# Log-softmax backward on one core: pairs of row groups, half of the sums on ScalarE, and a last store cut in three

## The chip, the core and the metric

The kernel runs on one core of a Trainium2 chip. The core has a vector engine (VectorE, DVE in the profile), a scalar engine (ScalarE, ACT), a general engine (GpSimd, POOL) and a sequencer that only issues transfers and waits (SyncE, SP). Sixteen DMA engines move data between the chip's large memory (HBM) and the core's working memory (SBUF), which has 128 partitions. The metric is device time in microseconds, the median of several executions. Before the change it is 1867.85 us over 9 executions (1866.99 to 1868.25).

## The reference

Inputs are `y` (the output of a log-softmax) and `dy`, each 8 x 1024 x 8192 float32. For each of the 8192 rows:

```
softmax_x = np.exp(y)
sum_dy = np.sum(dy, axis=-1, keepdims=True)
return (dy - softmax_x * sum_dy).astype(np.float32)
```

The two inputs and the output are 268.4 MB each, so 805 MB cross the DMA engines.

## The kernel before

The 8192 rows are cut into G = 32 groups of 256 rows. A group lies on the 128 partitions with R = 2 neighbouring rows per partition, so a partition's share of a group is 2 x 8192 elements, 64 KiB in one run of memory. The program is written out by one Python loop over the groups (L82); a framework inserts the semaphore waits, and each engine carries out its own instructions in the order of the program.

For one group:

- `load_dy` (L43) issues one 8 MiB load of dy into one of two buffers `dy_t` (L45). A `tensor_reduce` on VectorE (L47) sums both rows of every partition in one instruction and negates the sums into `s_t`.
- `load_y` (L56) issues two 4 MiB loads, one for each row of the pair, into two buffers `y_t` (L60). Each partition's piece is 32 KiB.
- `compute` (L64) goes over the two rows in halves of 4096 columns: ScalarE takes Exp in place in `y_t` (L69), then VectorE computes `e * (-sum) + dy` in one `scalar_tensor_tensor` into `dy_t` (L70).
- `store` (L74) writes the `dy_t` buffer back to `out` (L77), 8 MiB in one transfer.

All transfers are issued by SP, in this order once the loop runs: y of this group (two loads), dy of the next group, store of this group, y of the next group, and so on. SP is in order: it stands still at a transfer whose buffer isn't free or whose data isn't computed, and everything behind it in SP's program waits. The dy load of group g+1 takes the buffer of group g-1 and waits until that store has landed. The y loads wait until the computing of the group before has released the buffer.

At the end (L88 to L96) the store of the last but one group is held back and issued after the last y loads, and the last group is stored in two parts, one row of the pair each. The two dy buffers and two y buffers take 192 KiB of each partition.

Of the kernel before, what the change touches and what calls it, by code (L numbers as in the profile page):

```python
# [1 line left out]

# [5 lines left out]


EXP = mybir.ActivationFunctionType.Exp  # L10
ALU = mybir.AluOpType


@with_exitstack
def kernel(
    ctx: ExitStack,
    tc: tile.TileContext,
    y: bass.AP,
    dy: bass.AP,
    out: bass.AP,  # L20
):

    nc = tc.nc
    P = nc.NUM_PARTITIONS
    fp32 = mybir.dt.float32

    N, D = y.flatten_outer_dims().shape
    R = 2  # L30
    G = N // (P * R)
    assert N == G * P * R
    CD = D // 2

    y_v = y.flatten_outer_dims().rearrange("(g p r) d -> g p (r d)", p=P, r=R)
    dy_v = dy.flatten_outer_dims().rearrange("(g p r) d -> g p (r d)", p=P, r=R)
    out_v = out.flatten_outer_dims().rearrange("(g p r) d -> g p (r d)", p=P, r=R)

    dyp = ctx.enter_context(tc.tile_pool(name="dyp", bufs=2))
    yp = ctx.enter_context(tc.tile_pool(name="yp", bufs=R))  # L40
    stats = ctx.enter_context(tc.tile_pool(name="stats", bufs=2))

    def load_dy(g):  # L43
        dy_t = dyp.tile([P, R * D], fp32, name="dy_t")
        nc.sync.dma_start(out=dy_t[:], in_=dy_v[g])  # L45
        s_t = stats.tile([P, R], fp32, name="s_t")
        nc.vector.tensor_reduce(  # L47
            out=s_t[:],
            in_=dy_t[:].rearrange("p (r d) -> p r d", r=R),
            axis=mybir.AxisListType.X,  # L50
            op=ALU.add,
            negate=True,
        )
        return dy_t, s_t

    def load_y(g):  # L56
        y_ts = []
        for r in range(R):
            y_t = yp.tile([P, D], fp32, name="y_t")
            nc.sync.dma_start(out=y_t[:], in_=y_v[g][:, r * D : (r + 1) * D])  # L60
            y_ts.append(y_t)
        return y_ts

    def compute(dy_t, s_t, y_ts):  # L64
        for r in range(R):
            for c in range(0, D, CD):
                e = y_ts[r][:, c : c + CD]
                d = dy_t[:, r * D + c : r * D + c + CD]
                nc.scalar.activation(e, e, EXP)  # L69
                nc.vector.scalar_tensor_tensor(  # L70
                    out=d, in0=e, scalar=s_t[:, r : r + 1], in1=d, op0=ALU.mult, op1=ALU.add
                )

    def store(g, dy_t, parts=1):  # L74
        w = R * D // parts
        for k in range(parts):
            nc.sync.dma_start(  # L77
                out=out_v[g][:, k * w : (k + 1) * w], in_=dy_t[:, k * w : (k + 1) * w]
            )

    cur = load_dy(0)
    for g in range(G):  # L82
        if g < G - 1:
            y_ts = load_y(g)
            compute(*cur, y_ts)
            nxt = load_dy(g + 1)
            if g < G - 2:
                store(g, cur[0])  # L88
                cur = nxt
            else:  # L90
                held, cur = cur, nxt
        else:
            y_ts = load_y(g)
            compute(*cur, y_ts)
            store(g - 1, held[0])
            store(g, cur[0], parts=R)  # L96


# [1 line left out]
_INS = ['y', 'dy']  # L100
_OUTS = [((8, 1024, 8192), 'float32')]


# [23 lines left out]
```

## Time and profile before

| what | value |
|---|---|
| median of 9 executions | 1867.85 us |
| the profiled execution's own time | 1867.34 us |
| its span on the core | 1865.6 us |
| VectorE busy | 1119.2 us (60%) |
| ScalarE busy | 457.1 us (25%) |
| DMA engines' packet time | 100.0% of the span |
| mean rate | 432 GB/s |
| `tensor_reduce`, 128 x 16384 | 32 times, 17220 ns each |
| `scalar_tensor_tensor`, 128 x 4096 | 128 times, 4481 ns each |
| Exp, 128 x 4096 | 128 times, 3608 ns each |

The profile is taken by the hardware on one execution. "Busy" is time in which an engine carries out an instruction. A wait is put down to the work that ended it. The slices cut the span in 40 equal parts; a 9 stands for 90% busy or more. A transfer shows in two places: where SP issues it, and as packets on the 16 DMA engines[...]. The times of single packets are in the trace's packet records.

### The profile page before, as it was taken

What the parts mean: (1) busy time and instruction counts of PE and PEld (TensorE: products, weight loads), DVE (VectorE), ACT (ScalarE), POOL (GpSimd) and SP (SyncE); (2) the same over time, 40 slices, a digit from 0 to 9 for tenths busy, and PEclk for the clock granted to TensorE, in tenths of its full rate; (3) what the DMA queues carried; (4) which work ended last, traced back from release to release, by engine and by line L of the source; (5) the groups of instructions that cost most, each with busy time, mean ns of one, the idle gap of its engine ahead of it and who ended that gap; (6) DMA issues with size and microseconds to landing.
All of it is one profiled execution on the core that took longest, in us unless ns stands there. A gap on an engine that the chain in (4) does not pass through costs nothing.

```text
span 1865.6 us, 712 instructions
## 1 busy us (share of the span) xinstructions
DVE 1119.2 (60%) x160; ACT 457.1 (25%) x129; POOL 0.2 (0%) x4
## 2 busy tenths in 40 slices
DVE  5675555755557555575555755657656576565664
ACT  2023321233212332123321233212332113331132
POOL 0000000000000000000000000000000000000000
DMA  9999999999999999999999999999999999999999
GB/s 427 416 432 434 438 429 429 432 441 433 430 430 432 441 429 436 426 435 438 434 434 427 432 442 433 429 431 435 437 433 436 426 434 439 436 430 431 430 434 399
DMA packets 18582, 805.36 MB, mean 432 GB/s; under 512 B 2064, under 2 KB 2064, under 8 KB 2064
## 3 DMA queue, kind: packets, MB, share of 16 engines
q1 hardware_dynamic: 18576, 805.31, 100.0%
q14 instruction: 6, 0.05, 0.0%
HBM read 536.87 MB, written 268.44 MB: 432 GB/s over the span
## 4 chain that ended last, share of the span: by engine, by line
DMA 74%; DVE 17%; ACT 6%; SPq 1%; issue 1%; DVEq 0%; ACTq 0%
DMA y_t<-in_y_dram 69%; DVE dy_t L70 15%; ACT y_t L69 6%; DMA dy_t<-in_dy_dram 3%; DVE s_t L47 2%; DMA out_dram<-dy_t 1%; SPq L60 1%; SPq L77 1%; DVEq L122 0%; ACTq L69 0%; DVEq L70 0%
## 5 line engine op out<-in xcount | busy, mean ns | idle before, releaser
L70 DVE SCALAR_TENSOR_TENSOR dy_t<-y_t,s_t,dy_t 128x4096 f32<-128x4096 f32 x128 | 568.2, 4481 | 490.2 <-ACT y_t L69 490.0
L69 ACT ACTIVATE y_t<-y_t 128x4096 f32<-128x4096 f32 x128 | 455.9, 3608 | 1375.7 <-DMA y_t<-in_y_dram 1375.7
L47 DVE TENSOR_REDUCE s_t<-dy_t 128x2 f32<-128x16384 f32 x32 | 551.0, 17220 | 232.3 <-DMA dy_t<-in_dy_dram 232.3
L69 ACT ACT_TABLE_LOAD x1 | 1.3, 1283 | 0.7 <-PEq L111 0.7
L111 POOL MEMSET const-bfloat16-1.0<- 128x1 bf16 x1 | 0.1, 102 | 0.0
L111 POOL MEMSET const-uint8-127<- 128x1 uint8 x1 | 0.1, 102 | 0.0
L111 POOL MEMSET const-float32-0.0<- 128x1 f32 x1 | 0.1, 99 | 0.2 <-issue 0.2
L111 POOL MEMSET const-float32-1.0<- 128x1 f32 x1 | 0.1, 99 | 0.0
## 6 DMA issues: line engine op xcount, KB each, us to landing
y_t<-in_y_dram SPq DMA_DIRECT2D x64, 4096.0 KB, 35.9
out_dram<-dy_t SPq DMA_DIRECT2D x2, 4096.0 KB, 22.6
dy_t<-in_dy_dram SPq DMA_DIRECT2D x32, 38.7
out_dram<-dy_t SPq DMA_DIRECT2D x31, 26.1
```

Of the source, the lines that this page charges most:

```text
L47: nc.vector.tensor_reduce(out=s_t[:], in_=dy_t[:].rearrange("p (r d) -> p r d", r=R), axis=mybir.AxisListType.X, op=ALU.add, negate=True,)
L60: nc.sync.dma_start(out=y_t[:], in_=y_v[g][:, r * D : (r + 1) * D])
L69: nc.scalar.activation(e, e, EXP)
L70: nc.vector.scalar_tensor_tensor(out=d, in0=e, scalar=s_t[:, r : r + 1], in1=d, op0=ALU.mult, op1=ALU.add)
L77: nc.sync.dma_start(out=out_v[g][:, k * w : (k + 1) * w], in_=dy_t[:, k * w : (k + 1) * w])
L111: nc = _bacc.Bacc("TRN2", target_bir_lowering=False, num_devices=1)
```

## The change

The groups are taken in pairs. SP's order becomes: dy of the first group, y of the first group, dy of the second, y of the second, store of the first, store of the second. Details:

- There are two dy buffers, `x_ts[0]` for the first group of each pair and `x_ts[1]` for the second, and one y buffer of 2 x 8192 columns for both. Together they again take 192 KiB of each partition.
- y of the first group is one 8 MiB load, 64 KiB per partition. y of the second group is two 4 MiB loads, one for each row; each waits until that row of the first group has been computed, since it overwrites the same half of the y buffer.
- `sums`: VectorE sums the first row of each partition. ScalarE sums the second row, with two Copy instructions of 4096 columns that write into PSUM (their copy isn't used) and accumulate into `half_t`; a small VectorE instruction adds and negates the two halves.
- `compute` cuts a row into pieces of 2048, 3072 and 3072 columns in place of two of 4096.
- The very last store is issued as three transfers: partitions 0 to 14, partitions 15 to 126, and partition 127, whose 64 KiB are cut into 16 runs of 4 KiB.

The instructions on the engines: ScalarE carries out 64 Copies and 192 Exps (128 Exps before), VectorE 32 reduces of 8192 columns, 32 small adds and 192 `scalar_tensor_tensor` (32 reduces of 16384 and 128 before). SP issues 114 transfers (129 before).

```diff
+    PIECES = [(0, 2048), (2048, 5120), (5120, D)]
...
-    dyp = ctx.enter_context(tc.tile_pool(name="dyp", bufs=2))
-    yp = ctx.enter_context(tc.tile_pool(name="yp", bufs=R))
+    x_ts = [pool.tile([P, W], fp32, name=f"x{j}") for j in range(2)]
+    y_t = pool.tile([P, W], fp32, name="y_t")
+    copied = psum.tile([P, H], fp32, name="copied")
...
+    def sums(x):
+        s_t = stats.tile([P, R], fp32, name="s_t")
+        half_t = stats.tile([P, 2], fp32, name="half_t")
         nc.vector.tensor_reduce(
-            out=s_t[:],
-            in_=dy_t[:].rearrange("p (r d) -> p r d", r=R),
-            axis=mybir.AxisListType.X,
-            op=ALU.add,
-            negate=True,
+            out=s_t[:, 0:1], in_=x[:, :D], axis=mybir.AxisListType.X, op=ALU.add, negate=True
         )
+        for h in range(2):
+            nc.scalar.activation(
+                copied[:], x[:, D + h * H : D + (h + 1) * H], COPY, accum_out=half_t[:, h : h + 1]
+            )
+        nc.vector.tensor_scalar(
+            out=s_t[:, 1:2],
+            in0=half_t[:, 0:1],
+            scalar1=half_t[:, 1:2],
+            scalar2=-1.0,
+            op0=ALU.add,
+            op1=ALU.mult,
+        )
+        return s_t
...
+    def load_y(g, lo, hi):
+        nc.sync.dma_start(out=y_t[:, lo:hi], in_=y_v[g][:, lo:hi])
...
+    def compute(x, s_t, r):
+        for b, e in PIECES:
+            cs = slice(r * D + b, r * D + e)
+            nc.scalar.activation(y_t[:, cs], y_t[:, cs], EXP)
+            nc.vector.scalar_tensor_tensor(
+                out=x[:, cs],
+                in0=y_t[:, cs],
+                scalar=s_t[:, r : r + 1],
+                in1=x[:, cs],
+                op0=ALU.mult,
+                op1=ALU.add,
             )
...
+    for g in range(0, G, 2):
+        load_dy(g, x_ts[0])
+        load_y(g, 0, W)
+        s_t = sums(x_ts[0])
+        for r in range(R):
+            compute(x_ts[0], s_t, r)
+        load_dy(g + 1, x_ts[1])
+        s_t = sums(x_ts[1])
+        for r in range(R):
+            load_y(g + 1, r * D, (r + 1) * D)
+            compute(x_ts[1], s_t, r)
+        nc.sync.dma_start(out=out_v[g], in_=x_ts[0][:])
+        if g + 2 < G:
+            nc.sync.dma_start(out=out_v[g + 1], in_=x_ts[1][:])
         else:
+            nc.sync.dma_start(out=out_v[g + 1][0:15], in_=x_ts[1][0:15, :])
+            nc.sync.dma_start(out=out_v[g + 1][15 : P - 1], in_=x_ts[1][15 : P - 1, :])
+            nc.sync.dma_start(
+                out=out_v[g + 1][P - 1 : P].rearrange("p (e w) -> p e w", e=16),
+                in_=x_ts[1][P - 1 : P, :].rearrange("p (e w) -> p e w", e=16),
+            )
```

More of the change, by code (lines that the diff above doesn't have):

```diff
@@ L10 @@
 EXP = mybir.ActivationFunctionType.Exp
+COPY = mybir.ActivationFunctionType.Copy
 ALU = mybir.AluOpType
@@ L30 @@
     R = 2
+    W = R * D
     G = N // (P * R)
-    assert N == G * P * R
-    CD = D // 2
+    assert N == G * P * R and D == 8192 and G % 2 == 0
+    H = D // 2
+    PIECES = [(0, 2048), (2048, 5120), (5120, D)]
     y_v = y.flatten_outer_dims().rearrange("(g p r) d -> g p (r d)", p=P, r=R)
@@ L37 @@
     out_v = out.flatten_outer_dims().rearrange("(g p r) d -> g p (r d)", p=P, r=R)
-    dyp = ctx.enter_context(tc.tile_pool(name="dyp", bufs=2))
-    yp = ctx.enter_context(tc.tile_pool(name="yp", bufs=R))
[L41 to L45, printed above, removed]
+    pool = ctx.enter_context(tc.tile_pool(name="pool", bufs=1))
+    stats = ctx.enter_context(tc.tile_pool(name="stats", bufs=3))
@@ L46, in load_dy @@
+    psum = ctx.enter_context(tc.tile_pool(name="psum", bufs=1, space=bass.MemoryType.PSUM))
+    x_ts = [pool.tile([P, W], fp32, name=f"x{j}") for j in range(2)]
+    y_t = pool.tile([P, W], fp32, name="y_t")
+    copied = psum.tile([P, H], fp32, name="copied")
+    def load_dy(g, x):
+        nc.sync.dma_start(out=x[:], in_=dy_v[g])
+    def sums(x):
         s_t = stats.tile([P, R], fp32, name="s_t")
+        half_t = stats.tile([P, 2], fp32, name="half_t")
         nc.vector.tensor_reduce(
-            out=s_t[:],
@@ L49, in load_dy @@
-            in_=dy_t[:].rearrange("p (r d) -> p r d", r=R),
-            axis=mybir.AxisListType.X,
-            op=ALU.add,
-            negate=True,
-        )
-        return dy_t, s_t
-    def load_y(g):
-        y_ts = []
-        for r in range(R):
[L59 to L64, printed above, removed]
-        for r in range(R):
[L66 to L72, printed above, removed]
@@ L74, in store @@
-    def store(g, dy_t, parts=1):
-        w = R * D // parts
-        for k in range(parts):
+            out=s_t[:, 0:1], in_=x[:, :D], axis=mybir.AxisListType.X, op=ALU.add, negate=True
+        )
+        for h in range(2):
[10 more added lines that the diff above has]
+        )
@@ new lines @@
+    for g in range(0, G, 2):
+        load_dy(g, x_ts[0])
+        load_y(g, 0, W)
+        s_t = sums(x_ts[0])
+        for r in range(R):
+            compute(x_ts[0], s_t, r)
+        load_dy(g + 1, x_ts[1])
+        s_t = sums(x_ts[1])
+        for r in range(R):
+            load_y(g + 1, r * D, (r + 1) * D)
[3 more added lines that the diff above has]
+            nc.sync.dma_start(out=out_v[g + 1], in_=x_ts[1][:])
+        else:
+            nc.sync.dma_start(out=out_v[g + 1][0:15], in_=x_ts[1][0:15, :])
+            nc.sync.dma_start(out=out_v[g + 1][15 : P - 1], in_=x_ts[1][15 : P - 1, :])
@@ L77, in store @@
             nc.sync.dma_start(
-                out=out_v[g][:, k * w : (k + 1) * w], in_=dy_t[:, k * w : (k + 1) * w]
-            )
[L81 to L96, printed above, removed]
+                out=out_v[g + 1][P - 1 : P].rearrange("p (e w) -> p e w", e=16),
```

## The prediction

> **What bounds the kernel now.** I read the page's busy shares, slices and queues first, to see which resource is never idle.
>
> ```profile
> DVE 1119.2 (60%) x160; ACT 457.1 (25%) x129; POOL 0.2 (0%) x4
> ...
> DMA  9999999999999999999999999999999999999999
> ...
> DMA packets 18582, 805.36 MB, mean 432 GB/s; under 512 B 2064, under 2 KB 2064, under 8 KB 2064
> ## 3 DMA queue, kind: packets, MB, share of 16 engines
> q1 hardware_dynamic: 18576, 805.31, 100.0%
> q14 instruction: 6, 0.05, 0.0%
> ```
>
> The 16 DMA engines are busy for the whole span; VectorE and ScalarE are not. Then the waits of SP's queue, to see whether its waits starve the transfers:
>
> ```profile
> SPq L77 <- DVE dy_t L70: 985.5, 32, 35.0
> SPq L45 <- DMA out_dram<-dy_t: 742.8, 30, 25.4
> SPq L77 <- DMA dy_t<-in_dy_dram: 25.8, 2, 19.9
> ```
>
> SP waits long before every store and every dy load, yet the transfers never pause: each wait ends while the rings still hold earlier work. The timeline of one group shows how closely:
>
> ```profile
> 229.87 0.34 SPq L77 DMA_DIRECT2D out_dram<-dy_t  x1
> 230.30 0.86 SPq L60 DMA_DIRECT2D y_t<-in_y_dram  x2
> 237.28 17.22 DVE L47 TENSOR_REDUCE s_t<-dy_t 128x2 f32<-128x16384 f32 x1 [7.44 <-DMA dy_t<-in_dy_dram]
> 256.58 0.33 SPq L45 DMA_DIRECT2D dy_t<-in_dy_dram  x1
> ```
>
> The store is issued at 229.87 while the dy load ahead of it lands only at 237.28, some 7 us of cover. So the chain of waits, which names y loads for most of the span, follows the full rings, not a latency. Last, the end in windows of 1 us (columns: stretch, length, DVE, ACT, POOL, clock, DMA share, GB/s):
>
> ```profile
> 1860.00:1861.00 1.00, 0.00 (x0) 0.00 (x0) 0.00 (x0) 1.00 0.99 426
> 1861.00:1862.00 1.00, 0.00 (x0) 0.00 (x0) 0.00 (x0) 1.00 0.61 262
> 1862.00:1863.00 1.00, 0.00 (x0) 0.00 (x0) 0.00 (x0) 1.00 0.23 98
> 1863.00:1864.00 1.00, 0.00 (x0) 0.00 (x0) 0.00 (x0) 1.00 0.08 33
> ```
>
> The engines don't end together: the records put their last 16 completions at 1860.96 to 1864.35, spread evenly, the last 0.4 us after the next.
>
> From the packet records of the same trace: a 64 KiB packet takes 2.418 us (median), a 32 KiB one 1.213, so 2.426 for the same bytes. Per engine there are 504 of the first and 528 of the second: 504 x 2.418 + 528 x 1.213 = 1859.1 us. With the first packet's start at 1.7, its extra 0.75, and 1.2 after the last packet that is 1862.8; the span is 1865.6. The 2.8 left over is packets that ran long: in the first 18 groups or so the last dy packet ahead of a store takes up to 1 us more; summed over all groups that is 2.1 us per engine. Where engines have drifted apart (from about 1050 us) it vanishes.
>
> [...] This trace has 128-partition transfers alone, 65536 B / 2.418 us = 27.1 GB/s per engine[...]
>
> **The change, part by part.** Sums are against the profiled execution, 1867.34 us around its span of 1865.6; the median of the runs is 0.5 above it.
>
> *Order of loads and stores.* SP now issues per pair: dy, y whole, dy, y row 0, y row 1, store, store. In engine time (8 packets = 19.35, 16 halves = 9.7 per row of y) these fill 0 to 19.3, 38.7, 58.0, 67.7, 77.4, 96.8, 116.1. I allow 0.5 us from last packet to consumer (start of the kernel: about 22.0 to 22.49) and 1.0 from issue to first packet (0.73 to 1.73). An Exp of 2048 columns is about 1.9 (half of 3608 ns plus fixed part[...]). A row on VectorE is 2.3 + 3.4 + 3.4 = 9.1 (8.88 for two halves, plus one more fixed part).
> - y row 0 of the second group needs row 0 of the first computed: 38.7 + 0.5 + 1.9 + 9.1 = 50.2, first packet at 51.2, needed at 58.0: 6.8 spare. Row 1: ready at 60.3, needed at 67.7: 7.4 spare.
> - The second store needs the second group computed. Its sums: the half reduce is 17.22 / 2 = 8.6 from 59.3, ended by 68, as y row 0 lands at 68.2. Row 1 lands at 77.9, done 88.9, store ready at 89.9, needed at 96.8: 6.9 spare. Queued behind it on SP are the next pair's loads.
> - The next dy waits for the first store (97.3): ready at 98.3, needed at 116.1. The next y's buffer is free by then; the second dy (117.6) is needed at 154.8.
> So nothing starves: 0 us, hidden by the transfers ahead in the rings. If a wait came late by more than its 6.8 spare, each further us would cost 16 us over the pairs. What changes is the number of passages from loads to stores: 16 in place of 31. If they cost in proportion, 2.1 falls by 1.0; since the early ones are the dear ones, 0 to 1.5; I take 1.0.
>
> *y of even groups in 64 KiB runs.* 528 - 256 = 272 halves become 136 whole packets per engine: 136 x 0.008 = 1.1 us less. This is straight engine time, on the path.
>
> *Sums on ScalarE, three pieces per row.* ScalarE gets 64 Copies of about 3.6 (230 us) and 64 more fixed parts of 0.2; VectorE loses 32 x 8.6 = 275 and gains 32 small adds and 64 fixed parts, some 20. ScalarE ends near 700, VectorE near 865, both under the transfers: 0. SP issues 114 transfers in place of 129, 0.34 to 0.45 each, hidden in its waits. More instructions may mean more instruction fetches (6 now; around each, one engine fell 0.6 to 1.0 us back): +0.3 for the one that ends last, between 0 and 1.
>
> *The last store in three parts.* Issued together at about 90 of the last pair, behind a whole store, so their issue is covered. Without a limit at the ports: [...] Bounds -0.3 to +0.2; I take +0.1. With ports shared: [...] So +7 to +15.
>
> Sum without the port limit: -1.1 - 1.0 + 0.3 + 0.1 = -1.7, hence 1865.6 for an execution like the profiled one and 1866.2 for the median.
>
> **The rivals.**
> 1. *The ports bind in the last store* (ends slower). [...] Time 1866.2 + 7 to + 15 = 1873 to 1881. It decides from about +5.5 us, when the result passes 1871.6; it would show as a last stage of over 25 us.
> 2. *Fewer passages align everything* (faster). All of the 2.8 us left over goes, with the 1.1: 1867.85 - 3.9 = 1864.0. For it: the long packets lie at passages. Against: they fade after 18 of 31, so 16 passages may cost nearly as much.
> 3. *VectorE becomes late for the one y buffer.* Row work must grow by 6.8 us over 9.1 before anything is lost; the busy shares speak against it. At 9 us late, 16 x 2.2 = 35 us: 1901.
>
> **How the numbers follow.** Forecast (no limit at the ports): 0.45, own range 1864.3 to 1868.5. Ports: 0.40. Full alignment: 0.09. Late row or another wait: 0.06. About 0.2% (3.7 us) is what a measurement of this kernel tells from no change. Faster is rival 2, 0.09; slower is rivals 1 and 3, less the little of them under the bound, 0.45; same 0.46. The range leaves out the fastest few in a hundred and everything slower than the upper end of the ports: 1864.0 to 1880.5.
>
> **What would show it.** Right: DMA share full until the last 4 us, an end ring-down no longer than now, no wait of SP that leaves the DMA slices below 9, ScalarE near 700 us busy. Rival 1: the last 20 to 35 us run below 432 GB/s and long packets stand in the last store alone. Rival 3: dips every 116 us at the y loads. The prediction is wrong if long packets appear elsewhere, for instance if every passage now costs half a microsecond on all engines.

## The result and the profile after

The changed kernel takes 1883.84 us (median of 9 executions, 1880.53 to 1885.15), against 1867.76 us for the kernel before (29 executions). The ratio is 1.0082, 95% interval 1.0073 to 1.0090: some 15 us slower. The profiled execution took 1882.31 us around a span of 1880.5.

The profile page of the changed kernel: busy shares, the DMA slices with their rates, the packet counts and the queue.

```profile
DVE 859.9 (46%) x256; ACT 698.7 (37%) x321; POOL 0.2 (0%) x4
...
DMA  9999999999999999999999999999999999999998
GB/s 424 424 427 432 435 445 425 441 424 437 438 425 441 426 444 428 438 432 426 440 429 439 428 442 425 433 437 434 435 429 432 435 443 425 438 427 437 436 428 247
DMA packets 16151, 805.37 MB, mean 428 GB/s; under 512 B 1808, under 2 KB 1808, under 8 KB 1808
...
q1 hardware_dynamic: 16144, 805.31, 99.7%
```

39 slices run at the old rate. The last falls to 247 GB/s, where before it was 399. A slice is 1880.5 / 40 = 47 us, so the missing rate there is about (399 - 247) / 433 x 47 = 16 us of full transfer. The whole loss is at the very end.

The last part of the changed kernel in windows of 5 us (stretch, length, DVE, ACT, POOL, clock, DMA share, GB/s). A packet's time and bytes are counted in the stretch in which it starts:

```profile
1835.00:1840.00 5.00, 1.40 (x1) 0.00 (x0) 0.00 (x0) 1.00 0.97 419
1840.00:1845.00 5.00, 0.00 (x0) 0.00 (x0) 0.00 (x0) 1.00 1.80 262
1845.00:1850.00 5.00, 0.00 (x0) 0.00 (x0) 0.00 (x0) 1.00 0.42 170
1850.00:1855.00 5.00, 0.00 (x0) 0.00 (x0) 0.00 (x0) 1.00 0.97 301
1855.00:1860.00 5.00, 0.00 (x0) 0.00 (x0) 0.00 (x0) 1.00 0.93 288
1860.00:1865.00 5.00, 0.00 (x0) 0.00 (x0) 0.00 (x0) 1.00 0.92 328
1865.00:1870.00 5.00, 0.00 (x0) 0.00 (x0) 0.00 (x0) 1.00 0.72 223
```

The break is at 1840 us, where the last group's store reaches the DMA engines. They stay busy (share near 1 up to 1865; the 1.80 and 0.42 are long packets that began in the first of the two stretches), but they move 170 to 330 GB/s in place of 433. Engines that are busy and move less are engines whose packets take longer. In the packet records the first 16 or so packets from 1840.6 on take up to 12.5 us, and later ones often 3.5 to 5.3, where the 64 KiB packets just before this place take 2.418 us.

The middle of the kernel went as forecast. One pair of groups in the timeline of the changed kernel:

```profile
1681.59 9.25 SPq L75 DMA_DIRECT2D y_t<-in_y_dram  x2
...
1689.57 3.59 ACT L61 ACTIVATE copied<-x 128x4096 f32<-128x4096 f32 x1 [5.03 <-DMA x<-in_dy_dram]
...
1720.36 0.34 SPq L103 DMA_DIRECT2D out_dram<-x  x1
1728.24 0.34 SPq L52 DMA_DIRECT2D x<-in_dy_dram  x1
```

y row 0 is issued at 1681.59, 8.0 us before the dy load ahead of it lands (1689.57). The second store is issued at 1720.36, 7.9 us before the first store lands and releases the next dy load (1728.24). So the rings, the packets that wait on the DMA engines, never run dry: DMA stands at 9 in 39 of the 40 slices above.

### The profile page after: what moved, and what is told of

Its sections match the earlier page's. It is cut to its first block, busy times and chain, and to the rows that moved or that the text cites. A ratio compares the mean times of both kernels' runs of the same rounds, so it can differ in the third digit from the quotient of the medians.

```text
span 1880.5 us, 925 instructions
## 1 busy us (share of the span) xinstructions
DVE 859.9 (46%) x256; ACT 698.7 (37%) x321; POOL 0.2 (0%) x4
## 2 busy tenths in 40 slices
DMA packets 16151, 805.37 MB, mean 428 GB/s; under 512 B 1808, under 2 KB 1808, under 8 KB 1808
## 4 chain that ended last, share of the span: by engine, by line
DMA 64%; DVE 13%; ACT 10%; another core or an unknown queue 9%; issue 1%; SPq 0%; DVEq 0%; ACTq 0%
DMA x<-in_dy_dram 31%; DMA out_dram<-x 30%; DVE x L81 13%; ACT copied L61 6%; ACT y_t L80 4%; DMA y_t<-in_y_dram 3%; SPq L75 0%; DVEq L137 0%; ACTq L137 0%; SPq L52 0%; ACTq L80 0%; ACTq L61 0%
## 5 line engine op out<-in xcount | busy, mean ns | idle before, releaser
L81 DVE SCALAR_TENSOR_TENSOR x<-y_t,s_t,x 128x3072 f32<-128x3072 f32 (+1 forms) x192 | 579.5, 3059 | 255.4 <-ACT y_t L80 255.4
L57 DVE TENSOR_REDUCE s_t<-x 128x1 f32<-128x8192 f32 x32 | 277.8, 8682 | 721.1 <-DMA x<-in_dy_dram 721.1
L80 ACT ACTIVATE y_t<-y_t 128x3072 f32<-128x3072 f32 (+1 forms) x192 | 460.1, 2466 | 268.5 <-DMA y_t<-in_y_dram 241.0
L61 ACT ACTIVATE copied<-x 128x4096 f32<-128x4096 f32 x64 | 229.6, 3587 | 864.4 <-DMA x<-in_dy_dram 863.4
L61 ACT ACTIVATION_READ_ACCUMULATOR copied<-x 128x1 f32 x64 | 11.9, 186 | 0.0
L64 DVE TENSOR_SCALAR s_t<-half_t 128x1 f32<-128x1 f32 x32 | 6.5, 204 | 0.0
```

Of the source, the lines that this page charges most:

```text
L57: nc.vector.tensor_reduce(out=s_t[:, 0:1], in_=x[:, :D], axis=mybir.AxisListType.X, op=ALU.add, negate=True)
L61: nc.scalar.activation(copied[:], x[:, D + h * H : D + (h + 1) * H], COPY, accum_out=half_t[:, h : h + 1])
L64: nc.vector.tensor_scalar(out=s_t[:, 1:2], in0=half_t[:, 0:1], scalar1=half_t[:, 1:2], scalar2=-1.0, op0=ALU.add, op1=ALU.mult,)
L80: nc.scalar.activation(y_t[:, cs], y_t[:, cs], EXP)
L81: nc.vector.scalar_tensor_tensor(out=x[:, cs], in0=y_t[:, cs], scalar=s_t[:, r : r + 1], in1=x[:, cs], op0=ALU.mult, op1=ALU.add,)
```

## The experiments

Four theories stood at the start. *Ports*: a transfer's rate depends on which SBUF partitions go together in it, so the small parts of the last store are slow. That partitions share something called a port, and how many packets meet on one, was the author's assumption; the trace of the kernel before, with transfers of 128 partitions alone, shows neither. Its prices below are the author's estimates: multiples of the 2.418 us packet in that trace, with the multiple assumed. *Pairs*: the new order of loads and stores costs something. *Split*: each extra transfer costs a fixed time. *Engines*, the view that the forecast took, says that only rows per engine count, so the cutting is nearly free; its +0.1 us was an estimate too.

**Undo the cut.** The last group's store is one transfer, the rest as in the changed kernel.

```diff
-            nc.sync.dma_start(out=out_v[g + 1][0:15], in_=x_ts[1][0:15, :])
-            nc.sync.dma_start(out=out_v[g + 1][15 : P - 1], in_=x_ts[1][15 : P - 1, :])
-            ... (partition 127)
+            nc.sync.dma_start(out=out_v[g + 1], in_=x_ts[1][:])
```

> The changed kernel with its last group's store as one transfer of 128 partitions. Ports [...]: the whole loss lies in the three parts, so 1866.2 as in the sum without the port limit, and the last ring-down of about 4 us comes back. Pairs (the new order of loads and stores costs something that the profile hides): stays near 1884.

Measured 1867.55 us, ratio to the kernel before 0.9992 (0.9985 to 0.9998); 1.3 us above the 1866.2 of *Ports*. The end of its span in the same windows:

```profile
1850.00:1855.00 5.00, 0.00 (x0) 0.00 (x0) 0.00 (x0) 1.00 1.00 433
1855.00:1860.00 5.00, 0.00 (x0) 0.00 (x0) 0.00 (x0) 1.00 0.97 419
1860.00:1865.00 5.00, 0.00 (x0) 0.00 (x0) 0.00 (x0) 1.00 0.15 66
```

The rate is full until 1860, then the short ring-down. Three lines of the program carry the whole loss: 1883.84 - 1867.55 = 16.3 us. *Pairs* falls. Without them the rest of the change is worth 1.5 us (0.4 to 2.8) of 1868 by the ratio. Part of that is a tail of the kernel before: 8 of its 27 executions beside this run took over 1870 us, none of the 22 of this kernel. The medians, 1868.27 and 1867.55, differ by 0.7. Why the tail is gone stays open.

**The cut alone**, put into the kernel before in place of its last two-part store:

```diff
-            store(g, cur[0], parts=R)
+            x = cur[0]
+            (the three transfers: partitions 0 to 14, 15 to 126, 127)
```

> The kernel before, with only its last store in the three parts (15, 112, 1 partitions). Ports: 1867.8 + 15 = 1883, with long packets in the last 35 us alone. Pairs: 1868, since the order of the groups is as before.

Measured 1881.53 us, ratio 1.0070 (1.0051 to 1.0088): +13 us without any other part of the change, where 15 was expected.

```profile
1840.00:1845.00 5.00, 1.39 (x1) 0.00 (x0) 0.00 (x0) 1.00 2.01 328
1845.00:1850.00 5.00, 0.00 (x0) 0.00 (x0) 0.00 (x0) 1.00 0.09 39
1850.00:1855.00 5.00, 0.00 (x0) 0.00 (x0) 0.00 (x0) 1.00 0.83 315
1855.00:1860.00 5.00, 0.00 (x0) 0.00 (x0) 0.00 (x0) 1.00 1.16 367
```

The same sag as in the changed kernel; the 2.01 and 0.09 are again long packets that began in the first of the two stretches.

**Two halves.** From here to the crossing of the two sides each kernel is the one with the whole last store, and only that store is cut in another way.

```diff
-            nc.sync.dma_start(out=out_v[g + 1], in_=x_ts[1][:])
+            nc.sync.dma_start(out=out_v[g + 1][0:64], in_=x_ts[1][0:64, :])
+            nc.sync.dma_start(out=out_v[g + 1][64:128], in_=x_ts[1][64:128, :])
```

> The last store as partitions 0 to 63, then 64 to 127: every engine still has 8 rows. Ports: [...] each packet takes 4.84 us in place of 2.42 and the store 38.7 in place of 19.3: 1866.2 + 19.3 = 1885.5. Engines (only the rows per engine count): 1866.2. Split (a fixed cost per extra transfer, 16 us for two, so 8 each): 1874.

Measured 1885.47 us, ratio 1.0085 (1.0067 to 1.0103).

```profile
1845.00:1850.00 5.00, 0.00 (x0) 0.00 (x0) 0.00 (x0) 1.00 1.01 210
1850.00:1855.00 5.00, 0.00 (x0) 0.00 (x0) 0.00 (x0) 1.00 1.01 210
1860.00:1865.00 5.00, 0.00 (x0) 0.00 (x0) 0.00 (x0) 1.00 1.00 223
```

All 16 engines work (share 1.01, and the page counts 1808 completions, 16 for each of the 113 transfers), at half the rate: 210 GB/s in place of 433. The median packet takes 5.107 us, twice 2.418 and 6% more. *Engines* falls, and *split* is 11 us off. That the time hits the 1885.5 of *Ports* is partly luck: from the whole store it is +17.9 us, where eight packets of 5.107 us per engine would give +21.5. Between the two halves (about 1854 to 1861) many packets take under 4 us, as they would if packets of the two halves, in flight together, slowed each other less; that reason is argued.

**16 and 112.** No single row, and two parts whose partitions divide by 16.

```diff
+            nc.sync.dma_start(out=out_v[g + 1][0:16], in_=x_ts[1][0:16, :])
+            nc.sync.dma_start(out=out_v[g + 1][16:128], in_=x_ts[1][16:128, :])
```

> The last store as partitions 0 to 15, then 16 to 127; no single row, and every engine has 8 rows. Ports: [...] 1866.2 + 12 = 1878. Engines: 1866.2. Split: 1874. If the single row of the changed kernel were the costly part: 1867.

Measured 1883.08 us, ratio 1.0073 (1.0057 to 1.0088): +15.5 where the author's estimate was +12, so *Ports* has the direction right and the size 3.5 us too small. The single row isn't needed for the loss, nor is a part of 15 partitions.

**Eight transfers, neighbouring partitions or every eighth.** Both have the same count of transfers, of partitions per transfer and of bytes. Only which partitions go together differs.

```diff
+            for i in range(8):   # neighbouring
+                nc.sync.dma_start(out=out_v[g + 1][16 * i : 16 * i + 16], in_=x_ts[1][16 * i : 16 * i + 16, :])
```

```diff
+            for i in range(8):   # every eighth
+                nc.sync.dma_start(out=out_v[g + 1][i:P:8], in_=x_ts[1][i:P:8, :])
```

> The last store as eight transfers of 16 neighbouring partitions each, one row per engine and transfer. Ports: [...] 1867.6 + 58 = 1926[...]. Engines: 1867.6. Split (16 us for two extra transfers, so 8 each): 1867.6 + 56 = 1924.

> The last store again as eight transfers of 16 partitions, but every eighth partition: i, i + 8, and so on. Same count of transfers, of rows per engine and of bytes as with neighbouring partitions. Ports: [...] 4.84 to 5.1 us each, 38.7 to 41 in place of 19.3: 1867.6 + 19 to + 22 = 1887 to 1890. Engines: 1867.6. Split: 1924, as for neighbouring partitions.

Neighbouring: 1894.73 us, ratio 1.0147 (1.0133 to 1.0161). Every eighth: 1883.53 us, ratio 1.0085 (1.0071 to 1.0099). *Split* can't tell the two apart and is off by 29 and 40 us; it falls. *Ports* has the order right and the steps too dear: +27 for 58 or more, +16 for 19 to 22. The estimate let all engines move in step. In the packet records of the neighbouring cut most packets of the first transfer take 7.4 to 10.6 us, but four take 3.1 to 3.7, so the engines don't. Those that are done early may go on to the next transfer, whose partitions are others, and so spread the load. That reading is argued: the records don't say on which engine a packet ran, and no run isolates it.

**SBUF side or memory side.** The two cuts differ also in the addresses they write. So the sides were crossed: neighbouring partitions to every eighth row pair of the output, and the other way round.

```diff
-  out=out_v[g + 1][16 * i : 16 * i + 16], in_=x_ts[1][16 * i : 16 * i + 16, :]
+  out=out_v[g + 1][i:P:8], in_=x_ts[1][16 * i : 16 * i + 16, :]
```

> Eight transfers of 16 neighbouring SBUF partitions for the last store, but each goes to every eighth row pair of the output, so the last group's rows land in each other's places; bytes, transfers and rows per engine stay. Ports (the SBUF side decides): as with neighbouring partitions before, 1894.7. Memory side (the addresses written decide): as with every eighth partition, 1883.5.

> The other crossing: every eighth SBUF partition in each of the eight transfers, written to 16 neighbouring row pairs of the output, so again the last group's rows land in each other's places. Ports (the SBUF side decides): 1883.5. Memory side: 1894.7.

Measured 1895.02 us, ratio 1.0143 (1.0128 to 1.0158), and 1883.12 us, ratio 1.0079 (1.0062 to 1.0096). One stretch of each of the four, all with the same columns as above. Neighbouring partitions, to neighbouring rows:

```profile
1845.00:1875.00 30.00, 0.00 (x0) 0.00 (x0) 0.00 (x0) 1.00 0.89 188
```

Neighbouring partitions, to every eighth row pair:

```profile
1845.00:1875.00 30.00, 0.00 (x0) 0.00 (x0) 0.00 (x0) 1.00 0.87 188
```

Every eighth partition, to every eighth row pair:

```profile
1845.00:1875.00 30.00, 0.00 (x0) 0.00 (x0) 0.00 (x0) 1.00 0.97 229
```

Every eighth partition, to neighbouring row pairs:

```profile
1845.00:1875.00 30.00, 0.00 (x0) 0.00 (x0) 0.00 (x0) 1.00 0.93 225
```

The time follows the partitions read, within 0.5 us, and not the addresses written. The limit is on the SBUF side. How many partitions a transfer has is not what counts: 64 at a time cost +17.9 and 16 at every eighth +16.0, but 16 neighbouring ones +27.2. Why some partitions slow each other is not shown, nor is a cut of the whole store by partitions that would be free.

**A load.** The kernel with the whole last store, and one 4 MiB load of y (last group, second row) in two halves of the partitions.

```diff
+            if g + 2 == G and r == 1:
+                for lo in (0, 64):
+                    nc.sync.dma_start(out=y_t[lo : lo + 64, D:W], in_=y_v[g + 1][lo : lo + 64, D:W])
```

> The changed kernel with the whole last store, and one load (y of the last group, second row) as partitions 0 to 63, then 64 to 127. Ports in both directions: the 4 MiB take 19.4 to 20.4 in place of 9.7, and all that follows on the rings moves: 1867.6 + 9.7 to + 10.7 = 1877 to 1878. Ports for stores alone: 1867.6.

Measured 1880.44 us, ratio 1.0068 (1.0053 to 1.0083): +12.9.

```profile
1805.00:1810.00 5.00, 5.00 (x2) 3.44 (x1) 0.00 (x0) 1.00 0.99 426
1810.00:1815.00 5.00, 5.00 (x1) 3.98 (x4) 0.00 (x0) 1.00 1.08 341
1815.00:1820.00 5.00, 1.19 (x2) 0.00 (x0) 0.00 (x0) 1.00 1.02 197
1825.00:1830.00 5.00, 4.70 (x3) 3.32 (x2) 0.00 (x0) 1.00 1.03 216
```

Loads are halved as stores are: 32 KiB packets take 2.53 us (median) in place of 1.213. The loss is 2 to 3 us above the estimate; why stays open.

**y of the first group in 32 KiB pieces again**, with the whole last store.

```diff
-        load_y(g, 0, W)
+        for r in range(R):
+            load_y(g, r * D, (r + 1) * D)
```

> The changed kernel with the whole last store, and y of the first group of each pair also as two row loads (32 KiB pieces). Packet price (0.008 us for each 64 KiB in one piece): 256 halves more in place of 128 whole packets per engine, +1.0: 1868.6. No price: 1867.6.

Measured 1868.00 us, ratio 1.0000 (0.9992 to 1.0008), beside 0.9992 (0.9985 to 0.9998) with 64 KiB pieces. The ratios differ by 1.5 us in the expected direction and the medians by 0.45, but the intervals overlap, so the times alone don't settle 1 us. The packet records of the two kernels agree with the price. By their own medians, 640 x 2.418 + 256 x 1.215 = 1858.6 us per engine with 64 KiB pieces, and 512 x 2.418 + 512 x 1.214 = 1859.6 with halves. The mean of the 16 engines' last completions is 1861.5 and 1862.6. These are one execution each.

**Which part of the three.** Leave out the store of partitions 0 to 14, or that of partition 127, from the changed kernel.

```diff
-            nc.sync.dma_start(out=out_v[g + 1][0:15], in_=x_ts[1][0:15, :])
```

> The changed kernel without the store of partitions 0 to 14 of the last group (those 30 rows of the output are left out). Ports: what is left are 112 rows, seven per engine, that meet at some ports, and row pair 127 on one engine; [...] 1867.6 + 5 = 1872.5, so the first part is worth about 11 of the 16 us. If the 112 rows don't meet at ports: 1867.6. If the first part is nothing: 1884.

> The changed kernel without the store of partition 127 of the last group (2 rows of the output are left out). Its trace shows one completion and no 4 KiB packet for it, so it runs as one 64 KiB packet on one engine. Ports: between nothing and 2.4 us less than the changed kernel, 1881.4 to 1883.8. If the last part were the costly one: 1868.

Without the first part: 1869.20 us, ratio 1.0006 (0.9997 to 1.0014). Without the last: 1883.02 us, ratio 1.0069 (1.0048 to 1.0089). So the 15 partitions carry 1883.84 - 1869.20 = 14.6 of the 16.3 us. Partition 127 carries 0.8 by the medians and 2.4 by the ratios, whose intervals overlap: it is not told from nothing. The profile page of the kernel without the first part also tells how the transfers were laid out:

```profile
DMA packets 16121, 804.39 MB, mean 431 GB/s; under 512 B 1793, under 2 KB 1793, under 8 KB 1793
```

The small packets are the completions, 16 for each transfer of 128 partitions (2064 for 129 transfers in the kernel before). The changed kernel has 1808, and 1793 is 15 less: the first part ran on 15 engines. The packet records of the changed kernel agree, since at 1842.7 us fifteen packets of the first part are in flight at once. 1808 is 111 whole transfers x 16, plus 15, plus 16, plus 1: partition 127 ran as one 64 KiB packet on one engine. No packet of 4 KiB is there: the same 1808 packets are under 512 B and under 8 KB. The cut of the last row that the source writes never reached the engines.

## Why the prediction was wrong

**The step that failed** is "Without a limit at the ports", taken for the last store and priced at +0.1 us. It measured +16.3. The rival "The ports bind in the last store" gave 1873 to 1881; the time came 2.8 us above it, outside the range that ended at 1880.5. Of its cause the runs show that the loss goes with the partitions read; that a port is what binds is not shown.

**How the wrong value was chosen.** In the trace of the kernel before a 64 KiB packet takes 2.418 us, 27.1 GB/s per engine, and every transfer has 128 partitions. Such a trace can't tell a limit of the engines from one on the SBUF side that the partitions share. The forecast gave the cheap reading the edge with nothing in the profile for it. The runs tell the two apart: in two halves all 16 engines are busy and move 210 GB/s in place of 433, and the crossing shows that the partitions decide.

**The size of the rival.** Its +7 to +15 was the author's estimate; +16.3 was measured. Taking the first part away saves 14.6. The records say where that lies: of the 113 packets that follow, 46 take over 2.6 us behind the first part and 25 without it. So behind the first part more packets of the 112 rows are slow; that it does so by setting the engines out of step is argued. Those 112 rows and the last one, without the first part, take 1.6 us longer than the whole store, where the author's estimate was 5.

**Partition 127.** The source writes it as 16 runs of 4 KiB; it was one packet on one engine (1 completion of the 1808). Its weight in the result is small (0.8 us by the medians, not told from nothing).

**What held.** *Order of loads and stores*: 0 us. The working gave 8.3 us between the point at which y row 0 can be issued and the landing ahead of it, the trace has 8.0; for the second store 8.4, the trace has 7.9. *64 KiB runs*: -1.1 us was worked out, and 1.0 comes from the medians of the two kernels that differ in it alone. The working adds up durations, but in the records an engine's next packet starts 3 to 4 ns before the end of the one before. From start to start a 64 KiB packet takes 2.414 us and two halves 2.420 in the kernel before: the saving is then 0.8, and some 5.6 us of the span are left over where the working had 2.8. Of these 1.9 are no long packets, but the last engine's completion behind the mean of the 16 (1864.35 and 1862.49). *Engines off the path*: ScalarE 698.7 us for some 700, VectorE 859.9 for some 865. An Exp of 2048 columns took 1905 ns where about 1.9 us stood and one of 3072 took 2747, so by the two lengths some 0.22 us of each is fixed; a row on VectorE took 2.35 + 6.75 = 9.1 us, as worked out. One instruction was not in the sum; the groups of the changed kernel show it:

```profile
L61 ACT ACTIVATE copied<-x 128x4096 f32<-128x4096 f32 x64 | 229.6, 3587 | 864.4 <-DMA x<-in_dy_dram 863.4
L61 ACT ACTIVATION_READ_ACCUMULATOR copied<-x 128x1 f32 x64 | 11.9, 186 | 0.0
```

Each accumulating Copy is followed by a read of the accumulator, 186 ns, 11.9 us in all, hidden under the transfers.

**A small miss with no effect.** "Passages" from loads to stores were to save 1.0 us, being 16 in place of 31. In the packet records what long packets cost in mid-run, as a mean per engine, is 2.17 us before and 2.07 with the whole last store: half the passages cost about the same. The forecast's lower bound, 0, was the right value. So the sum without the ports was -1.7 and the kernel with the whole store measured -1.5 (-2.8 to -0.4) by the ratio. That near hit is partly luck: with the passages at nothing the sum is -0.7, as the medians have it, and the rest is the tail of the kernel before.

## What to carry to other kernels

In a kernel bound by transfers, don't cut a transfer by partitions as it was cut here: parts of 64, 16 or 15 partitions were slow here while all or most of the 16 engines were busy, and 8 MiB in two halves of the partitions took nearly twice as long (about 37 us for 19). If a transfer has to be cut, cut it along the columns, as the kernel before does with its last store: there the rate stays at 426 GB/s from 1855 to 1860 us, 5 us before the end. Before trusting a cut that is meant to balance engines, count its completions in the profile: here they showed 15 for 15 partitions, 16 for 112 and 1 for the single one.

## What the runs showed that was not expected

- In a store cut in two halves of the partitions the median 64 KiB packet takes 5.107 us, 6% more than twice the 2.418 us of the whole store; in a load cut so, 32 KiB packets go from 1.213 to 2.53.
- In the first transfer of 16 neighbouring partitions packets took from 3.1 to 10.6 us. Eight such transfers cost +27 us, not the +58 of the author's estimate.
- A row of 64 KiB that the source cuts into 16 runs of 4 KiB was moved as one packet by one engine.
